# A hybrid trunk layer on one core: the opening laid out anew, and the operands of phase B made one by one

## The chip, the cores and the metric

One core of one Trainium2 chip runs the whole kernel. The metric is the device time of one execution in microseconds; the time of a kernel is the median over its runs.

## The reference

The layer normalises 16 learned meta tokens and 1024 tokens of width 2048, multiplies them with one combined weight `w_in` (2048 x 10240), and cuts the result into queries, keys, values, gates, the input of a pooling mixer, and two merge gates:

```python
h = rmsnorm(x, gain)
zin = h @ w_in.astype(h.dtype)
q, k, v, g_attn, u, g_pool, m_attn, m_pool = jnp.split(zin, cuts, axis=-1)
o_attn = stick_breaking_attention(q, k, v).reshape(B, L, SB_WIDTH)
y_attn = (o_attn * silu(g_attn)) @ w_attn_up
mixed = einsum(multiscale_pool(u), pool_w)
y_pool = (mixed * pool_scale * silu(g_pool)) @ w_pool_up
merged = sigmoid(m_attn) * y_attn + sigmoid(m_pool) * y_pool
return x + merged @ w_out
```

A second RMS norm with `final_gain` follows. The change touches only the way in which `zin` is computed; everything behind it is as before.

## The kernel before, in words

**Products.** Each fp32 operand is split into a hi and a lo part (`split`, L115: hi on ACT, lo on DVE or POOL), and a product is three matmuls: hi by hi, hi by lo, lo by hi (`mm3`, L137 to L140). The weight's parts are the tiles `wh` and `wl` (four buffers each, two products' worth), the tokens' parts are the X tiles.

**Pairs.** Two column blocks of 128 of `w_in` make a pair (class `Duo`); there are 40. The tokens are cut into two halves of 512 and the 2048 rows of the weight into two halves, and a pair's result is made with seven block products in place of eight, over sums of blocks. Phase A, per pair, does four products of 24 matmuls of 128x512: X0, X2, X1 and X3 are token-side operands. X0 and X1 hold the first half of the tokens, X2 and X3 differences with the last half. A pair's weight blocks arrive as four `raw` tiles of 512 KB (`load_raw`, L207; the first index `kh` is the half of the rows); POOL makes eight sums of them (`make_sums`, L221: r1 to r4, two of each), of which r2 and r3 go into X2's and X3's products, and r1 and r4 are stored to `d_r` for phase B. Phase B does the other three products of a pair, with operands Y0, Y1, Y2, which are other sums of token blocks.

**Opening (L271 to L408).** Eight blocks of 128 tokens and the 16 meta tokens are loaded, normed (`norm_block`, L276) and transposed on PE 128x128 at a time (`turn`, L314, tile `xtr`). Blocks 0 to 3 and meta become X0 and X1 (`first_tokens`). Blocks 4 to 7 go through `last_tokens` (L333): e22 (a scaled transpose, stored to `d_x22`), t3 (a difference), t2 (X0 less t3, two operations on POOL), then the splits of t3 into X3 and of t2 into X2. It is called 16 times with 256 columns: for blocks 4 and 5, then for blocks 6 and 7. The tiles of blocks 4 to 7 and of meta share two `xt` buffers in pool `p0`. Two pairs run in the opening: their X0 and X1 products between the steps of the norm, their X2 and X3 products at the end. Raw tiles and sums of these pairs come from `p0` too; the loop's come from pool `wa`, which opens when `p0` is closed.

**Loop (L441 to L464).** The other 38 pairs follow, with the next pair's raw tiles (raw0 four buffers, raw1 two) loaded and summed during the present pair. In eight of them `second_operands` (L418) makes 512 columns of two of phase B's operands on DVE: it fetches `d_x22` into an `st` tile (L422), subtracts X2, stores `d_t1`; and a second `st` tile gets a chain of three subtractions and additions that begins at L427, and is stored to `d_t4`. The same four `st` buffers carry the pairs' results to `d_nu`, `d_up`, `d_sa` and `d_sp`.

**Into phase B (L474 to L487).** 24 tiles of 512 columns are read back from `d_t1`, `d_t4` and `d_x22` through the four `wr` buffers and split, all of Y0, Y1 and Y2, before `duo` (L491) is called for the first pair.

**What sets the order.** A scheduler places each engine's instructions, which then run in that order and wait for semaphores. All DMAs are issued by one engine, SyncE, in its own order, and one that waits for a buffer holds back those behind it.

## Time and profile before

| | us |
|---|---|
| median of 3 runs | 2665.68 |
| lowest, highest run | 2661.87, 2668.41 |
| profiled execution, its time | 2664.01 |
| profiled execution, its span | 2662.3 |
| PE busy in the span | 2521.7 |
| phase A's last product ends | 1028.9 |
| phase B's first product starts | 1045.24 |

The profile is one execution; times count from the start of its span. PE is the matmul engine, DVE, ACT and POOL the elementwise ones, SP the one that issues the DMAs. A group of instructions is named by its line, engine, operation and tiles (without buffer numbers, so that r1 to r4 all read `r`), and idle time in front of an instruction is put down to what released it.

### The profile page before, as it was taken

The page shows a single profiled execution, that of the slowest core. Times are in us where ns is not written, and L with a number is a line of the kernel's source. Part 1 is how long each engine was busy: PE and PEld are TensorE (multiplying, and loading weights), DVE is VectorE, ACT ScalarE, POOL GpSimd, SP SyncE. Part 2 cuts the span into 40 slices and gives each one's busy share as a digit, 9 for nine tenths or more (in the row PEclk, how much of TensorE's full clock was granted, in tenths as well). Part 3 has the DMA queues.
Part 4 walks back from the last instruction along what each step waited for, and adds up shares of the span by engine and source line. Part 5 has one row for each costly group of instructions (what it writes and reads, how often), then busy time and mean ns, then how long its engine had stood idle before and what let it go on. Part 6 is the DMA issues. An engine that isn't in the chain of part 4 may idle for free.

```text
span 2662.3 us, 36486 instructions
## 1 busy us (share of the span) xinstructions
PE 2521.7 (95%) x12968; PEld 2123.3 (80%) x12968; DVE 1306.1 (49%) x2183; ACT 950.4 (36%) x1929; POOL 881.2 (33%) x802
## 2 busy tenths in 40 slices
PE   6589899999999997999999999999999999999998
PEld 5368677888888886888888888888778888788888
DVE  6643434343333345575665566556744424544432
ACT  5422222222222224324555454545532223322331
POOL 3555344554455452334323322333201101211010
PEclk9799999999999998999999999999999999999999
DMA  5455655555555556544334433433394434564431
GB/s 193 145 176 179 207 185 181 182 178 175 178 178 178 178 163 196 162 131 151 119 120 127 120 119 126 125 118 100 112 285 144 143 103 141 184 201 143 146 101 64
DMA packets 386775, 409.88 MB, mean 154 GB/s; under 512 B 34064, under 2 KB 262416, under 8 KB 385552
## 3 DMA queue, kind: packets, MB, share of 16 engines
q1 hardware_dynamic: 386592, 407.54, 48.4%
q8 instruction: 102, 1.67, 0.3%
q14 instruction: 81, 0.66, 0.1%
HBM read 298.17 MB, written 109.28 MB: 153 GB/s over the span
## 4 chain that ended last, share of the span: by engine, by line
PE 77%; DMA 6%; POOL 5%; DVE 5%; issue 3%; ACT 2%; SPq 1%; DVEq 0%; POOLq 0%; ACTq 0%
PE acc L138 15%; PE acc L139 15%; PE acc L140 15%; PE accb L826 4%; PE accb L825 4%; PE accb L824 4%; POOL r L226 4%; PE accb L140 4%; PE accb L138 4%; PE accb L139 4%; DMA raw<-in_w_in_dram 2%; PE tr L644 1%; DMA st<-d_x 1%; DVE bt L629 1%; PE av L139 1%
## 5 line engine op out<-in xcount | busy, mean ns | idle before, releaser
L138 PE MATMUL acc<-x,wh 128*128 128x512 f32 (+2 forms) x2736 | 979.0, 358 | 30.6 <-ACT wh L116 24.0
L140 PE MATMUL acc<-x,wl 128*128 128x512 f32 (+2 forms) x2736 | 975.4, 357 | 21.2 <-DVE wl L117 21.2
L139 PE MATMUL acc<-x,wh 128*128 128x512 f32 (+2 forms) x2736 | 975.2, 357 | 1.7 <-DVE x L117 1.7
L138 PEld LDWEIGHTS acc<-x,wh 128*128 128x128 f32 x2736 | 519.7, 190 | 106.2 <-ACT wh L116 26.7
L140 PEld LDWEIGHTS acc<-x,wl 128*128 128x128 f32 x2736 | 519.0, 190 | 101.7 <-DVE wl L117 28.2
L139 PEld LDWEIGHTS acc<-x,wh 128*128 128x128 f32 x2736 | 519.3, 190 | 72.6 <-DVE x L117 3.8
L116 ACT ACTIVATE wh<-wr 128x512 fp32r<-128x512 f32 x480 | 302.2, 630 | 512.2 <-PE accb L139 166.5
L117 DVE TENSOR_TENSOR wl<-wr,wh 128x512 fp32r<-128x512 f32 x360 | 258.9, 720 | 274.8 <-ACT wh L116 265.3
L117 POOL TENSOR_TENSOR wl<-wr,wh 128x512 fp32r<-128x512 f32 x120 | 171.3, 1427 | 364.6 <-ACT wh L116 265.5
L226 POOL TENSOR_TENSOR r<-raw,raw 128x512 f32<-128x512 f32 x80 | 115.2, 1440 | 411.5 <-DMA raw<-in_w_in_dram 390.6
L226 POOL TENSOR_TENSOR r<-r,raw 128x512 f32<-128x512 f32 x160 | 232.0, 1450 | 14.1 <-DMA raw<-in_w_in_dram 4.9
L116 ACT ACTIVATE wh<-r 128x512 fp32r<-128x512 f32 x160 | 101.0, 632 | 376.1 <-PE acc L139 183.8
L117 DVE TENSOR_TENSOR wl<-raw,wh 128x512 fp32r<-128x512 f32 x152 | 131.0, 868 | 207.0 <-ACT wh L116 192.7
L117 DVE TENSOR_TENSOR wl<-r,wh 128x512 fp32r<-128x512 f32 x160 | 151.1, 945 | 155.3 <-ACT wh L116 154.9
L140 PE MATMUL accb<-x,wl 128*128 128x512 f32 x512 | 201.2, 393 | 2.8 <-DVE wl L117 2.8
L138 PE MATMUL accb<-x,wh 128*128 128x512 f32 x512 | 200.9, 392 | 2.3 <-ACT wh L116 2.3
L139 PE MATMUL accb<-x,wh 128*128 128x512 f32 x512 | 200.2, 391 | 0.0
L116 ACT ACTIVATE wh<-raw 128x512 fp32r<-128x512 f32 x160 | 100.5, 629 | 244.1 <-PE acc L139 213.1
L826 PE MATMUL accb<-wl,x 128*128 128x512 f32 x448 | 175.9, 393 | 0.7 <-DVE wl L117 0.7
L824 PE MATMUL accb<-wh,x 128*128 128x512 f32 x448 | 175.8, 392 | 0.0
L825 PE MATMUL accb<-wh,x 128*128 128x512 f32 x448 | 175.7, 392 | 0.0
L816 POOL TENSOR_TENSOR sa<-sa,sp 128x512 f32<-128x512 f32 x32 | 51.0, 1592 | 319.4 <-DVE sa L815 310.1
(167 smaller groups left out, 3042.9 us busy)
## 6 DMA issues: line engine op xcount, KB each, us to landing
raw<-in_w_in_dram SPq DMA_DIRECT2D x104, 512.0 KB, 5.2
d_r<-r SPq DMA_DIRECT2D x160, 256.0 KB, 2.0
wr<-d_r SPq DMA_DIRECT2D x160, 256.0 KB, 2.9
raw<-in_w_in_dram SPq DMA_DIRECT2D x128, 256.0 KB, 5.3
wr<-in_w_out_dram SPq DMA_DIRECT2D x128, 256.0 KB, 2.6
wr<-in_w_in_dram SPq DMA_DIRECT2D x80, 256.0 KB, 3.0
wr<-in_w_pool_up_dram SPq DMA_DIRECT2D x64, 256.0 KB, 3.8
wr<-in_w_attn_up_dram SPq DMA_DIRECT2D x64, 256.0 KB, 3.4
```

The costliest lines, as they stand in the source:

```text
L116: nc.scalar.activation(hi, src, AF.Copy)
L117: (eng or nc.vector).tensor_tensor(out=lo, in0=src, in1=hi.bitcast(F32), op=ALU.subtract)
L138: nc.tensor.matmul(ps, wh, rh, start=first, stop=False, skip_group_check=skip)
L139: nc.tensor.matmul(ps, wh, rl, start=False, stop=False, skip_group_check=skip)
L140: nc.tensor.matmul(ps, wl, rh, start=False, stop=last, skip_group_check=skip)
L226: nc.gpsimd.tensor_tensor(out=t, in0=a, in1=b, op=ALU.add)
L629: nc.vector.tensor_tensor(out=bt[:, :w], in0=bt[:, :w], in1=wt[:, 1 : w + 1], op=ALU.mult)
L644: nc.tensor.transpose(tr[:, n, :], bt[:, off : off + P], ident)
L816: nc.gpsimd.tensor_tensor(out=sa, in0=sa, in1=sps.pop(c), op=ALU.add)
L824: nc.tensor.matmul(a, sh, wh, start=k == 0, stop=False)
L825: nc.tensor.matmul(a, sl, wh, start=False, stop=False)
L826: nc.tensor.matmul(a, sh, wl, start=False, stop=k == KC - 1)
```

## The change

1. The opening's `xt` tiles get a pool of their own, `px`, with four buffers, for blocks 4 to 7 and meta (five loads). `last_tokens` runs 8 times with 512 columns in place of 16 times with 256. Its tiles e22 and t2 have one buffer each, t3 is a `wr` tile, and the first operation on t2 moves from POOL to DVE. The squares' junk goes to `wr` tiles.
2. Three pairs run ahead in place of two. Their X0 and X1 products come first, with `last_tokens` put in between those of pairs 1 and 2 (two calls behind each half of their X1 products); the copies s1 of the first products are held in `wr` tiles. Their X2 and X3 products follow, with sums from `wa`, which takes the place of `px` in memory.
3. All raw tiles come from one pool `ws` and, for the last of a pair's four, from `wa`: raw0 has two buffers, raw1 one, rawb one.
4. `second_operands` works in `wr` tiles, and its `d_x22` is fetched one pair earlier by `fetch_x22`.
5. Y0, Y1 and Y2 are each made when `duo` first asks for them (`operand(n)`).

The diff, cut to its core:

```diff
-            def load_raw(pool, d, kh, kq, bufs):
-                raw = pool.tile([P, QD, 2 * P], F32, tag=f"raw{kh}", name=nm("raw"), bufs=bufs)
+            def load_raw(d, kh, kq, pool=None):
+                if pool is None:
+                    raw = ws.tile([P, QD, 2 * P], F32, tag=f"raw{kh}", name=nm("raw"), bufs=2 - kh)
+                else:
+                    raw = pool.tile([P, QD, 2 * P], F32, tag="rawb", name=nm("raw"), bufs=1)
...
+            early = ALL[:3]
...
-                        xt = p0.tile([P, D], F32, tag="xt", name=nm("xt"), bufs=2)
+                        xt = px.tile([P, D], F32, tag="xt", name=nm("xt"), bufs=4)
...
+                def last_tokens(r):
+                    tb, _ = turn(g2, r + KC // 2)
+                    e22 = p0.tile([P, HALF], F32, tag="e22", name=nm("e22"), bufs=1)
...
+                    t3 = wr_tile()
...
+                    t2 = p0.tile([P, HALF], F32, tag="t2", name=nm("t2"), bufs=1)
-                    nc.gpsimd.tensor_tensor(out=t2, in0=bh, in1=t3, op=ALU.subtract)
+                    nc.vector.tensor_tensor(out=t2, in0=bh, in1=t3, op=ALU.subtract)
                     nc.gpsimd.tensor_tensor(out=t2, in0=t2, in1=bl, op=ALU.add)
...
-                g2 = [norm_block(4), norm_block(5)]
+                g2 = [norm_block(b) for b in range(HB, NB)]
...
+                for d in early[1:]:
+                    early_ops(d, 0)
+                    a = acc_tile()
+                    for kq in range(KQ):
+                        block([a], WHOLE, X0, kq, ops[d.n, 0, kq], True)
+                    s1[d.n] = wr_tile()
+                    nc.scalar.activation(s1[d.n], a, AF.Copy)
+                    early_ops(d, 1)
+                    for kq in range(KQ):
+                        block([a], WHOLE, X1, kq, ops[d.n, 1, kq], False)
+                        for i in range(2):
+                            last_tokens(4 * (d.n - 1) + 2 * kq + i)
+                    out_c(p0, 2, d, [a], WHOLE)
...
-                return [[load_raw(wa, d, kh, kq, 4 - 2 * kh) for kq in range(KQ)] for kh in range(2)]
+                return [[load_raw(d, 0, 0), load_raw(d, 0, 1)], [load_raw(d, 1, 0), load_raw(d, 1, 1, wa)]]
+
+            for d in early:
+                raws = all_raws(d)
+                r2, r3 = make_sums(wa, d, raws, SB)
...
-                t = st_tile(wa, STB)
-                nc.sync.dma_start(t, d_x22[r])
+                t = x22s.pop(r)
...
-                t = st_tile(wa, STB)
+                t = wr_tile()
                 nc.vector.tensor_tensor(out=t, in0=f[1][0], in1=f[2][0], op=ALU.subtract)
...
+                if 3 <= n < 3 + KC // 2:
+                    fetch_x22(n - 3)
...
-            prod(c, pieces, Y0, lambda kq: d_r[d.n][0][:, kq * 512 : (kq + 1) * 512], True)
+            prod(c, pieces, operand(0), lambda kq: d_r[d.n][0][:, kq * 512 : (kq + 1) * 512], True)
...
-            prod(n4, pieces, Y1, lambda kq: w_in[krows(1, kq), d.c1 : d.c1 + P].rearrange("(k p) c -> p k c", p=P), True)
+            prod(n4, pieces, operand(1), lambda kq: w_in[krows(1, kq), d.c1 : d.c1 + P].rearrange("(k p) c -> p k c", p=P), True)
```

The order of the instructions at three places follows. First ACT in the opening, from the last squares of the norm on. `junk` is the squares of a block, `rs` the root of its norm, `wh` the hi part of a weight, `e22`, `t3` and `t2` the tiles of `last_tokens`, `st` and `wr` copies of results. Before, from the squares of block 5:

```order
L298 ACTIVATE junk_106_783,ssq_105_781<-xt_104_780 128x1024
L298 ACTIVATE junk_107_785,ssq_105_781<-xt_104_780 128x1024
L116 ACTIVATE wh_134_907<-raw_132_904 128x512
L149 ACTIVATE rs_109_790<-var_108_788 128x1
L245 ACTIVATE st_119_884<-acc_112_799 128x512
L263 ACT_TABLE_LOAD
L263 ACTIVATE st_120_886<-acc_69_572 128x256
L263 ACTIVATE st_120_886<-acc_70_573 128x256
L339 ACTIVATE e22_136_913<-xtr_135_910,gk_404 128x256
```

Now, from the squares of block 7:

```order
L309 ACTIVATE junk_122_827,ssq_121_825<-xt_120_824 128x1024
L309 ACTIVATE junk_123_829,ssq_121_825<-xt_120_824 128x1024
L267 ACT_TABLE_LOAD
L267 ACTIVATE st_128_891<-acc_70_579 128x256
L149 ACT_TABLE_LOAD
L149 ACTIVATE rs_125_834<-var_124_832 128x1
L116 ACTIVATE wh_139_906<-raw_137_903 128x512
L116 ACTIVATE wh_142_912<-raw_140_909 128x512
L116 ACTIVATE wh_147_945<-raw_145_942 128x512
L116 ACTIVATE wh_150_951<-raw_148_948 128x512
L388 ACTIVATE wr_144_940<-acc_143_915 128x512
L348 ACTIVATE e22_152_971<-xtr_151_966,gk_407 128x512
```

The first weights of pair 1 (`wh_139`) stand behind all of block 7's norm; before, pair 1's first weights were split earlier, ahead of the first row shown.

Second POOL, where the last tokens and the sums of the first pairs meet. Before:

```order
L226 TENSOR_TENSOR r2_260_1372<-r3_259_1370,raw_257_1366 128x512
L226 TENSOR_TENSOR r1_261_1374<-raw_255_1362,raw_257_1366 128x512
L226 TENSOR_TENSOR r4_262_1376<-r2_260_1372,raw_257_1366 128x512
L346 TENSOR_TENSOR t2_196_1130<-x0_1_393,t3_195_1128 128x256
L347 TENSOR_TENSOR t2_196_1130<-t2_196_1130,x0_2_394 128x256
L346 TENSOR_TENSOR t2_201_1148<-x0_1_393,t3_200_1146 128x256
L347 TENSOR_TENSOR t2_201_1148<-t2_201_1148,x0_2_394 128x256
L346 TENSOR_TENSOR t2_206_1166<-x0_1_393,t3_205_1164 128x256
L347 TENSOR_TENSOR t2_206_1166<-t2_206_1166,x0_2_394 128x256
```

Now, the sums being those of pair 0:

```order
L356 TENSOR_TENSOR t2_190_1147<-t2_190_1147,x0_4_399 128x512
L356 TENSOR_TENSOR t2_195_1169<-t2_195_1169,x0_4_399 128x512
L230 TENSOR_TENSOR r3_211_1248<-raw_207_1240 128x512
L230 TENSOR_TENSOR r1_213_1252<-raw_207_1240,raw_209_1244 128x512
L230 TENSOR_TENSOR r2_212_1250<-r3_211_1248,raw_209_1244 128x512
L230 TENSOR_TENSOR r3_215_1258<-raw_208_1242 128x512
L230 TENSOR_TENSOR r4_214_1254<-r2_212_1250,raw_209_1244 128x512
L356 TENSOR_TENSOR t2_200_1203<-t2_200_1203,x0_4_399 128x512
L230 TENSOR_TENSOR r2_216_1260<-r3_215_1258,raw_210_1246 128x512
L230 TENSOR_TENSOR r1_217_1262<-raw_208_1242,raw_210_1246 128x512
L230 TENSOR_TENSOR r4_218_1264<-r2_216_1260,raw_210_1246 128x512
L356 TENSOR_TENSOR t2_205_1225<-t2_205_1225,x0_4_399 128x512
```

The subtraction of t2 has left POOL, and the last two of its eight additions stand behind five and three of pair 0's sums.

Third ACT at the step into phase B (`x0`, `x1`, `x2` are now Y0, Y1, Y2; `wr` and `ym` what is read back). Before:

```order
L116 ACTIVATE x1_1632_8744<-wr_1668_8870 128x512
L116 ACTIVATE x1_1632_8744<-ym_1669_8874 128x16
L481 ACTIVATE x2_1634_8746<-wr_1670_8878 128x512
L481 ACTIVATE x2_1634_8746<-wr_1671_8882 128x512
L481 ACTIVATE x2_1634_8746<-wr_1672_8886 128x512
L481 ACTIVATE x2_1634_8746<-wr_1673_8890 128x512
L481 ACTIVATE x2_1636_8748<-wr_1674_8894 128x512
L481 ACTIVATE x2_1636_8748<-wr_1675_8898 128x512
L481 ACTIVATE x2_1636_8748<-wr_1676_8902 128x512
L481 ACTIVATE x2_1636_8748<-wr_1677_8906 128x512
L116 ACTIVATE pwh_1678_8916<-wr_1680_8918 128x512
L116 ACTIVATE wh_1689_8935<-wr_1687_8932 128x512
```

Now:

```order
L116 ACTIVATE wh_1588_8608<-r3_1563_8460 128x512
L116 ACTIVATE x0_1601_8666<-wr_1615_8716 128x512
L116 ACTIVATE x0_1601_8666<-wr_1617_8724 128x512
L116 ACTIVATE x0_1601_8666<-ym_1618_8728 128x16
L116 ACTIVATE wh_1621_8735<-wr_1619_8732 128x512
L116 ACTIVATE x1_1628_8798<-ym_1633_8806 128x16
L116 ACTIVATE x1_1628_8798<-ym_1635_8814 128x16
L116 ACTIVATE wh_1624_8765<-wr_1622_8762 128x512
L267 ACTIVATE st_1584_8600<-acc_1568_8497 128x512
L116 ACTIVATE x1_1628_8798<-wr_1632_8802 128x512
```

Phase B's first weights (`wh_1689` before, `wh_1621` now) stand right behind the last tiles of Y0, and Y1's tiles behind them.

More of the change, by code (lines that the diff above doesn't have):

```diff
@@ L294, in norm_block @@
                     for i, hh in enumerate(halves):
-                        on_act = i == 0 or b not in (0, 1)
-                        junk = p0.tile([P, D // 2], BF16, tag="junk" if on_act else "st", name=nm("junk"), bufs=1 if on_act else 3)
-                        if on_act:
+                        junk = wp.tile([P, D // 2], BF16, tag="wr", name=nm("junk"), bufs=4)
+                        if i == 0 or b not in (0, 1):
                             nc.scalar.activation(junk[:n], xt[:n, hh], AF.Square, accum_out=ssq[:n, i : i + 1])
@@ L349, in last_tokens @@
-                    split(X2[kq][0][:, j, cs], X2[kq][1][:, j, cs], t2)
-                early = ALL[:2]
+                    split(X3[kq][0][:, j], X3[kq][1][:, j], t3)
+                    split(X2[kq][0][:, j], X2[kq][1][:, j], t2)
                 half = [range(0, KC // 2), range(KC // 2, KC)]
                 g0 = [norm_block(0), norm_block(1)]
-                ops = {}
-                raws = {}
-                def early_ops(d, kh):
-                    for kq in range(KQ):
-                        raw = load_raw(p0, d, kh, kq, 2 - kh)
-                        ops[d.n, kh, kq] = op_of(c0(raw), nc.gpsimd)
@@ L398, in trunk_kernel @@
[L398 to L402 removed]
+                out_c(p0, 2, early[0], A0, SPLIT)
+                X2, X3 = xquads(2, HALF), xquads(3, HALF, xp)
+                for d in early[1:]:
+                    early_ops(d, 0)
+                    a = acc_tile()
@@ L472, in load_wr, with operand @@
             return raw
-        Y0, Y1, Y2 = xquads(0, XW), xquads(1, XW), xquads(2, HALF)
-        for Y, src, neg in ((Y0, d_t1, False), (Y1, d_t4, False), (Y2, d_x22, True)):
+        Y = {}
+        def operand(n):
+            if n in Y:
+                return Y[n]
+            Y[n] = xquads(n, XW if n < 2 else HALF)
+            src = (d_t1, d_t4, d_x22)[n]
             for r in range(KC // 2):
@@ L523, in duo @@
             out_of((1, 0), n4, up, False)
-            prod(c, SPLIT if d.meta else WHOLE, Y2, lambda kq: d_r[d.n][1][:, kq * 512 : (kq + 1) * 512], False)
+            prod(c, SPLIT if d.meta else WHOLE, operand(2), lambda kq: d_r[d.n][1][:, kq * 512 : (kq + 1) * 512], False)
             out_of((0, 1), c, nu, True)
```

77 lines of the change are left out of this document (29 added, 48 removed).

## The prediction, made before the result was known

> **What bounds the kernel now.** I read the page's busy table first, then the sums over stretches, then the waits of PE, then PE's timeline at the longest waits.
>
> ```profile
> span 2662.3 us, 36486 instructions
> ...
> PE 2521.7 (95%) x12968; PEld 2123.3 (80%) x12968; DVE 1306.1 (49%) x2183; ACT 950.4 (36%) x1929; POOL 881.2 (33%) x802
> ```
>
> PE is busy for 2521.7 of 2662.3 us, and the change takes no matmul of the products away. So all it can give lies in the 140.6 us in which PE stands idle, and in what the lower clock behind such gaps costs. Where these lie, the sums over stretches tell (the columns are PE, PEld, DVE, ACT, POOL busy, granted PE clock, DMA share, GB/s):
>
> ```profile
> 50.30:75.00 24.70, 17.61 (x80) 12.89 (x78) 14.55 (x23) 13.58 (x29) 17.38 (x17) 0.90 0.47 152
> 75.00:101.30 26.30, 4.78 (x18) 3.15 (x18) 18.53 (x31) 12.36 (x26) 16.81 (x17) 0.51 0.60 188
> 101.30:143.70 42.40, 28.43 (x112) 18.60 (x112) 18.08 (x34) 10.18 (x24) 15.70 (x18) 0.98 0.31 106
> 262.10:489.70 227.60, 208.37 (x866) 164.72 (x865) 91.05 (x130) 53.27 (x90) 101.69 (x74) 0.98 0.56 190
> 489.70:1005.00 515.30, 515.30 (x2779) 445.04 (x2778) 200.35 (x230) 140.86 (x266) 267.62 (x187) 1.00 0.56 175
> 1005.00:1055.00 50.00, 33.63 (x168) 28.77 (x167) 26.89 (x55) 25.00 (x56) 4.98 (x5) 0.83 0.73 224
> ```
>
> Three places lose time, and the change touches all three: the opening (7.1, 21.5 and 14.0 us idle up to 143.7), the pairs from 262 to 490 (19.2 us), and the step into phase B (16.4 us). From 490 to 1005 PE never waits. PE's waits over the whole run, then its timeline at the gaps (idle time and releaser in brackets):
>
> ```profile
> PE xtr L320 <- DVE xt L308: 36.8, 5, 16.1
> PE acc L138 <- ACT wh L116: 24.0, 3, 16.4
> PE acc L140 <- DVE wl L117: 21.2, 14, 2.4
> ```
>
> ```profile
> 91.95 1.09 PE L320 MATMUL xtr<-ident,xt 128*128 128x128 f32 x4 [16.10 <-DVE xt L308]
> 97.64 3.01 PE L320 MATMUL xtr<-ident,xt 128*128 128x128 f32 x12 [4.60 <-DVE xt L308]
> ...
> 143.74 0.79 PE L138 MATMUL acc<-x,wh 128*128 128x512 f32 x1 [7.36 <-ACT wh L116]
> ...
> 168.59 0.40 PE L138 MATMUL acc<-x,wh 128*128 128x512 f32 x1
> ...
> 217.69 0.40 PE L138 MATMUL acc<-x,wh 128*128 128x512 f32 x1
> ...
> 239.90 0.40 PE L138 MATMUL acc<-x,wh 128*128 128x512 f32 x1
> ...
> 489.66 0.29 PE L138 MATMUL acc<-x,wh 128*128 128x256 f32 x1
> ...
> 1028.47 0.40 PE L140 MATMUL acc<-x,wl 128*128 128x512 f32 x1
> 1045.24 0.58 PE L138 MATMUL acc<-x,wh 128*128 128x256 f32 x1 [16.37 <-ACT wh L116]
> ```
>
> The rows without a bracket are starts of pairs: pair 3 at 168.59, pairs 5 and 6 at 217.69 and 239.90 (an undisturbed pair takes 22.21 us, a product 5.55), the first u pair, number 16, at 489.66. The sum below is made against the profiled execution, 2664.0 us; the median of the runs lies 1.7 us above it, well inside their spread of 6.5.
>
> **Part 1, the opening: 20 us.** The waits of 16.10 and 4.60 us are for blocks 6 and 7, whose loads stand behind the two shared buffers. With four buffers blocks 4 to 6 come early, and block 7 takes the buffer of meta. In the chain of waits of before block 5's load stands so, and ACT at that time:
>
> ```profile
> 46.64 5.81 DMA xt<-in_x_dram
> ```
>
> ```profile
> 52.53 1.06 ACT L298 ACTIVATE junk<-xt 128x1024 bf16<-128x1024 f32 x1 [2.86 <-DMA xt<-in_x_dram]
> 53.50 0.19 ACT L298 ACTIVATION_READ_ACCUMULATOR junk<-xt 128x1 f32 x1
> 56.71 1.28 ACT L263 ACT_TABLE_LOAD   x1
> ```
>
> The last of four blocks lands about where block 5 does now, near 52.5. Its squares now stand on ACT ahead of pair 1's first operands: two times 1.25, two table loads of 1.28, a copy, a root and the split (0.63 by a row below) put that split's end near 59. PE has only transposes from 50.5 until then, so this is a new wait of some 6.5 us; pair 1's first product ends near 66. Then last_tokens runs in 8 rounds of 512 columns. One t2 buffer makes the rounds a chain, which I price by the 512-column rows of 50 to 147 us, and 256-column ones beside them:
>
> ```profile
> L346 POOL TENSOR_TENSOR t<-x,t 128x256 f32<-128x256 f32 x16 | 13.6, 852 | 8.0 <-DVE t L343 8.0
> L226 POOL TENSOR_TENSOR r<-r,raw 128x512 f32<-128x512 f32 x8 | 11.8, 1481 | 0.2 <-DMA raw<-in_w_in_dram 0.2
> ...
> L117 DVE TENSOR_TENSOR wl<-r,wh 128x512 fp32r<-128x512 f32 x8 | 8.2, 1030 | 3.7 <-ACT wh L116 3.6
> L343 DVE SCALAR_TENSOR_TENSOR t<-xtr,gk,e 128x256 f32<-128x256 f32 x16 | 7.2, 475 | 2.0 <-ACT e L339 2.0
> ...
> L116 ACT ACTIVATE wh<-r 128x512 fp32r<-128x512 f32 x8 | 4.9, 625 | 6.5 <-PE acc L139 5.0 <-POOL r L226 1.4
> ```
>
> A round is subtract 1.03 (DVE, moved there from POOL), add 1.48 (POOL), hi 0.63 (ACT), lo 1.03 (DVE) and four hand-overs of 0.2, so 5.0 us. The 0.2 is the gap in this row of DVE:
>
> ```profile
> 101.30 0.66 DVE L117 TENSOR_TENSOR x<-t,x 128x256 fp32r<-128x256 f32 x1 [0.20 <-ACT x L116]
> ```
> The first t3 is there near 68, and the add of the sixth round ends near 95.5. Then POOL has five sums of pair 0 (7.4 us), the add of round 7, three more sums (4.4) and the add of round 8, which ends near 110; hi and lo follow, and pair 0's X2 product ends near 113, its X3 at 118.5. SyncE's queue has the fourth raw tile of pair 0 behind the last transposes, but POOL is still busy when it lands. Pairs 1 and 2 are paced by load, sums and product in turn. A raw tile takes 4.8 us to land:
>
> ```profile
> raw<-in_w_in_dram SPq DMA_DIRECT2D x62, 512.0 KB, 4.8
> d_r<-r SPq DMA_DIRECT2D x63, 256.0 KB, 2.0
> ```
>
> The first raws of a pair wait for the sums of the one before, its last one also for the nu store. So pair 1's two products end near 131, pair 2's X2 starts near 134.5 (2 sums after its raws), and its X3 ends near 147, in place of 168.59. That is 21.6; I take 20, for half clock behind one more gap. Bounds: 8 if each round costs 1.5 us more (a POOL operation in between), and 47 if only PE were left (10 products of 5.55 and 64 transposes of 0.25 after 50.3 end at 122). The value lies near the low end because the chain of rounds is known by its rows.
>
> A rule speaks of that clock. After the wait of 7.36 us the first matmul takes 0.79 us, and 0.40 in pair 5. The Trainium skill (TensorE: Matmul & The Clock Gate, What's actually happening) says that an idle window of about 3.4 us halves the clock, until one such window has been busy. By it each of my three gaps (59, 100, 134) would cost up to 1.7 us, an estimate from that page, and the end would be 3.4 us later than mine; the trace agrees on the halving and not on the length, since 4.60 us of idle near 97 were followed by a stretch at 0.98.
>
> **Part 2, pairs 3 to 15: 31 us.** From 168.59 to 489.66 stand 321.1 us; thirteen undisturbed pairs are 288.7, so 32.4 are lost, in the nine pairs of 262 to 490 above all (25.3 each). DVE waits there:
>
> ```profile
> DVE wl L117 <- ACT wh L116: 52.7, 31, 2.5
> DVE st L427 <- DMA d_sp<-st: 35.7, 4, 9.1
> DVE st L427 <- DMA d_sa<-st: 34.7, 4, 8.8
> ```
>
> L427 is the first subtraction of t4 in second_operands: it waits for an st tile whose store is late, 8.8 us each time, and the lo splits of the next products stand behind it on DVE; PE then waits for wl 14 times. With wr tiles that wait has no object, since a slot comes round after two rounds, and d_x22 is fetched a pair ahead. What is late next would be the raws, and they have slack: the four wl buffers let X1's operands be split two products ahead, so raw1 is free near +5 and +7.5 us of a pair and lands again near +12.3; its sums (six of 1.48) are done near +21.2, and the next pair's r2 is needed at 22.2 + 5.6 = 27.8. So 22.2 us a pair; I leave 1.4 of 32.4 for one slow clock window. Bounds 15 (second operands still cost half) and 33.
>
> **Part 3, into phase B: 9 us.** The last X3 ends at 1028.9, the next product starts at 1045.24: 16.4 us idle, and 2.3 (an estimate: some 5 us of work at half clock, by the 0.83 granted there), 18.7 lost. In that stretch:
>
> ```profile
> L116 ACT ACTIVATE x<-wr 128x512 fp32r<-128x512 f32 x16 | 10.0, 625 | 6.4 <-DMA wr<-d_t 4.7 <-PE acc L140 1.8
> L481 ACT ACTIVATE x<-wr 128x512 fp32r<-128x512 f32 x8 | 5.0, 630 | 5.4 <-DMA wr<-d_x 5.3
> ```
>
> 24 tiles go through ACT before the first weights: 15.0 us of work and 11.8 of waiting for loads, 1.1 us a tile. After, the first weights stand behind 8 tiles only, which are ready before X3 ends. The other 16 need 1.1 us each, or 1.5 (four thirds of it) while pool_w holds one of four wr slots, from about 1027 on: 1045 to 1051. PE's three products of 5.6 need until 1046, and each waits for the tiles of its operand. The third product ended near 1064 (1045.24, three of 5.6, 2.3 for the clock); now it ends between 1047 and, with a last half product and a slow clock behind the last tile, 1055. I take 1055, since every load of these tiles shares SyncE's queue: 9. Bounds 3 (the tiles wait on each other as now) and 17.
>
> Costed at nothing: the junk of the squares in wr tiles, which nothing else uses by then, and the doubled raw of the first three pairs, which POOL's earlier work hides; if that cover is gone, it is in the 1.5 us a round of part 1's lower bound.
>
> **Sum.** 20 + 31 + 9 = 60: 2664.0 - 60 = 2604, and 2605 against the median.
>
> **The rivals.**
>
> *DVE and POOL block each other (0.12).* The lo split takes 1.03 us here, beside 0.69 where POOL rests:
>
> ```profile
> L117 DVE TENSOR_TENSOR x<-wr,x 128x512 fp32r<-128x512 f32 x16 | 11.0, 688 | 5.4 <-ACT x L116 5.2
> ```
>
> If each of three two-input DVE operations in a round (t2 and two lo) had to wait for a whole POOL one, 1.48 in place of the mean 0.34, 8 rounds would take 8 x 3 x 1.14 = 27 us more, and 20 gained become 7 lost: 2632. Against it speaks that mean, a quarter of an operation. The Trainium skill (SBUF — State Buffer, Who interferes with whom) states this rule for two-input DVE operations beside POOL reads, the later one fully blocked; the trace agrees on some operations only.
>
> *The second operands still block (0.15).* The scheduler pulls them into pairs 3 to 7, and DVE now waits for the d_x22 fetch instead. A third of part 2 remains: 2625. For it: the SyncE queue is in order. Against it: the fetch is issued early.
>
> *Slower: the single raw buffers (0.07).* If a raw tile lands later than 11.4 us after issue (4.8 and the slack of 6.6 us, 27.8 less 21.2), every one of 37 pairs waits. At the 3.1 us that a disturbed pair loses now (25.3 less 22.2), 37 pairs lose 115: 2719. Against it: the raws landed in 4.8.
>
> *The opening near PE's own time (0.06).* Rounds that overlap: 27 us more, 2577.
>
> *It does not do what it says (0.05).* The chain of rounds and the sums behind it take back what the other parts give: about 2660.
>
> **How the numbers follow.** The forecast has 0.55; the range 2585 to 2635 holds it with its bounds and the first two rivals, 0.82, and leaves out the last three. A measurement can tell about 0.3%, 8 us, from no change. Faster by more: 0.55 + 0.12 + 0.15 + 0.06 = 0.88; within: 0.05; slower: 0.07.
>
> **What would show it.** Right: in the changed profile no wait for xt of over 3 us near 90; PE starts pair 3 near 147; pairs 3 to 15 take 22.2 us; no gap near 1029, and waits of 10 us in all until 1055. Wrong: waits of PE for r or raw in every pair, DVE rows of 1.5 us and more in the rounds, or a wait for wl in pairs 3 to 7.

## The result, and the profile after

| | us | ratio to before (95% interval) |
|---|---|---|
| before, median | 2667.05 (2661.87 to 2669.29) | |
| after, median of 4 runs | 2625.99 (2621.62 to 2632.07) | 0.985 (0.9825 to 0.9875) |
| profiled execution of after, its time and span | 2632.07, 2630.4 | |

The kernel became faster by 41 us in the medians and by 31.9 us between the two profiled spans; the profile after is of the slowest of its four executions. One execution of a repeat of after took 3110 us at a granted clock of 0.749, and no figure below contains it. The result lies in the range, 21 us above the forecast of 2605. The page of after begins so:

```profile
span 2630.4 us, 36376 instructions
...
PE 2522.7 (96%) x12968; PEld 2130.9 (81%) x12968; DVE 1317.9 (50%) x2163; ACT 948.8 (36%) x1907; POOL 883.4 (34%) x782
```

PE does the same work (2522.7 us, before 2521.7), so the gain is idle time. The stretches of after, cut nearly as those of before (PE, PEld, DVE, ACT, POOL busy, granted PE clock, DMA share, GB/s):

```profile
0.00:50.30 50.30, 30.26 (x149) 24.05 (x149) 30.65 (x83) 30.27 (x68) 6.56 (x10) 0.83 0.66 222
50.30:75.00 24.70, 17.41 (x80) 13.45 (x80) 11.63 (x26) 16.30 (x28) 7.32 (x6) 0.79 0.41 120
75.00:101.30 26.30, 22.10 (x111) 17.86 (x109) 17.26 (x23) 13.60 (x23) 12.91 (x9) 0.94 0.52 171
101.30:120.00 18.70, 8.59 (x21) 5.54 (x21) 18.00 (x18) 5.44 (x10) 16.05 (x12) 0.73 0.59 193
...
170.00:262.00 92.00, 78.71 (x313) 62.31 (x312) 62.33 (x86) 19.09 (x33) 40.38 (x27) 0.93 0.63 208
262.00:490.00 228.00, 228.00 (x1033) 187.20 (x1032) 93.01 (x103) 61.68 (x107) 123.70 (x85) 1.00 0.53 178
...
1005.00:1037.30 32.30, 23.07 (x150) 22.20 (x150) 19.77 (x31) 15.50 (x28) 5.24 (x4) 0.84 0.84 265
```

From 75 to 101 PE now works 22.1 us where it worked 4.8, and from 262 to 490 it never waits. But two holes have grown: 10.1 us idle from 101 to 120 (5.7 in before), and 13.3 us idle from 170 to 262 (2.7 in before). PE's timeline at the starts of pair 4 (180.39), pair 7 (267.03) and the first u pair, number 16 (466.95), with the gaps between and behind them:

```profile
62.49 0.80 PE L138 MATMUL acc<-x,wh 128*128 128x512 f32 x1 [2.52 <-ACT wh L116]
...
107.23 0.79 PE L138 MATMUL acc<-x,wh 128*128 128x512 f32 x1 [6.47 <-ACT wh L116]
...
180.39 0.40 PE L138 MATMUL acc<-x,wh 128*128 128x512 f32 x1
194.23 0.65 PE L140 MATMUL acc<-x,wl 128*128 128x512 f32 x1 [2.18 <-DVE wl L117]
...
218.33 0.79 PE L140 MATMUL acc<-x,wl 128*128 128x512 f32 x1 [3.44 <-DVE wl L117]
...
253.65 0.80 PE L140 MATMUL acc<-x,wl 128*128 128x512 f32 x1 [5.79 <-DVE wl L117]
...
267.03 0.40 PE L138 MATMUL acc<-x,wh 128*128 128x512 f32 x1
...
466.95 0.29 PE L138 MATMUL acc<-x,wh 128*128 128x256 f32 x1
...
1015.99 0.38 PE L138 MATMUL acc<-x,wh 128*128 128x256 f32 x1 [4.00 <-ACT wh L116]
1029.09 0.58 PE L138 MATMUL acc<-x,wh 128*128 128x256 f32 x1 [5.23 <-ACT wh L116]
...
1037.14 0.40 PE L138 MATMUL acc<-x,wh 128*128 128x512 f32 x1
```

The last row is the fourth product of phase B; in before it stood here:

```profile
1064.75 0.40 PE L138 MATMUL acc<-x,wh 128*128 128x512 f32 x1
```

Pairs 7 to 15 take 466.95 - 267.03 = 199.9 us, nine times 22.21, the undisturbed pair. Pair 3 ran without a gap, so its start is put at 180.39 - 22.21 = 158.2 (its X0 product is interleaved with the opening's last). That gives the parts:

| | before | after | gain | forecast |
|---|---|---|---|---|
| opening, until pair 3 starts | 168.6 | 158.2 | 10.4 | 20 |
| pairs 3 to 15 | 321.1 | 308.8 | 12.3 | 31 |
| first u pair until phase A's last product ends (1028.86, 1006.15) | 539.2 | 539.2 | 0 | 0 |
| step into phase B, until its fourth product | 35.9 | 31.0 | 4.9 | 9 |
| the rest | 1597.5 | 1593.3 | 4.3 | 0 |

The last row is no work of the change. From the matmul at 1141.9 in before to the start of the last one stand 1511.5 us; the same stretch, counted in matmuls from the end, takes 1507.5 in after and from 1507.2 to 1512.4 in the other kernels profiled below, with 1508.1 in the fastest of all and 1511.3 in the one from which it differs by a queue.

Pairs 3 to 6 take 108.8 us and not 88.8: 20 us are lost there, 13.3 of them idle time and the rest the slow clock behind it (0.65 to 0.80 us for a matmul of 0.40 in the rows above). What DVE and then SyncE's queue wait for, from 160 to 270:

```profile
DVE tm L437 <- DMA d_t<-tm: 15.6, 4, 6.5
DVE wr L426 <- DMA wr<-d_x: 8.4, 1, 8.4
```

```profile
SPq L239 <- POOL r L230: 47.6, 19, 4.8
```

L426 and L437 are lines of `second_operands`: its first subtraction, from the fetched d_x22, and the sum of 16 meta columns in a `tm` tile, of which there are four. SyncE at L239 issues the stores of r1 and r4 to `d_r`, and each waits in the queue for POOL's sum. The sums in turn wait for raw loads out of the same queue (51.6 us in four waits of POOL, from 160 to 270). Two single waits show the chain, first DVE, then SyncE's queue before the second of them:

```profile
192.07 0.18 DVE L437 TENSOR_TENSOR tm<-x,x 128x16 f32<-128x16 f32 x1 [6.47 <-DMA d_t<-tm]
...
251.57 1.42 DVE L426 TENSOR_TENSOR wr<-wr,x 128x512 f32<-128x512 f32 x2 [8.41 <-DMA wr<-d_x]
```

```profile
242.64 0.32 SPq L239 DMA_DIRECT2D d_r<-r  x1
...
245.05 0.38 SPq L216 DMA_DIRECT2D raw<-in_w_in_dram  x1
245.49 0.68 SPq L419 DMA_DIRECT2D wr<-d_x  x1
```

The fetch that DVE needs at 243.2 is issued only at 245.49, behind the stores and raw loads, and lands 6 us later. DVE stands still, with lo splits of the next product behind it.

### The profile page after: what moved, and what is told of

Read it like the earlier page. It is cut to its first block, busy times and chain, and to the rows that moved or that the text cites. A ratio compares the mean times of both kernels' runs of the same rounds, so it can differ in the third digit from the quotient of the medians.

```text
span 2630.4 us, 36376 instructions
## 1 busy us (share of the span) xinstructions
PE 2522.7 (96%) x12968; PEld 2130.9 (81%) x12968; DVE 1317.9 (50%) x2163; ACT 948.8 (36%) x1907; POOL 883.4 (34%) x782
## 4 chain that ended last, share of the span: by engine, by line
PE 81%; DVE 4%; issue 2%; DMA 2%; ACT 1%; POOL 0%; DVEq 0%; SPq 0%; POOLq 0%; ACTq 0%
PE acc L139 17%; PE acc L138 17%; PE acc L140 17%; PE accb L837 4%; PE accb L836 4%; PE accb L835 4%; PE accb L138 4%; PE accb L140 4%; PE accb L139 4%; PE tr L655 1%; DVE bt L640 1%; PE av L139 1%; PE av L140 1%; DVE wt L639 1%; PE av L138 1%
## 5 line engine op out<-in xcount | busy, mean ns | idle before, releaser
L230 POOL TENSOR_TENSOR r<-r,raw 128x512 f32<-128x512 f32 x160 | 248.0, 1550 | 11.6 <-DMA raw<-in_w_in_dram 3.1
```

Of the source, the lines that this page charges most:

```text
L230: nc.gpsimd.tensor_tensor(out=t, in0=a, in1=b, op=ALU.add)
```

## The experiments

The medians of all runs, with the start of the first u pair in each profile (before 489.66, after 466.95). Before was run again beside each, at 2663 to 2667.

| kernel | median us | ratio (95% interval) | first u pair |
|---|---|---|---|
| after, repeated (3 runs) | 2629.51 | 0.9873 (0.985 to 0.9895) | |
| before with part 5 alone | 2661.15 | 0.9987 (0.9975 to 0.9998) | 497.06 |
| before with part 4 alone | 2647.92 | 0.9929 (0.9904 to 0.9954) | 477.63 |
| after without parts 4 and 5 | 2650.73 | 0.9938 (0.9918 to 0.9958) | 479.78 |
| after, 16 tm buffers | 2633.33 | 0.9894 (0.987 to 0.9918) | 463.89 |
| after, d_r stored by POOL | 2631.08 | 0.9877 (0.9858 to 0.9895) | 462.93 |
| after, packed raw tile | 2623.12 | 0.9845 (0.983 to 0.9859) | 458.94 |
| packed, two rawb buffers | 2635.56 | 0.9885 (0.987 to 0.9899) | 468.85 |
| packed, second operands' DMAs by ACT | 2629.9 | 0.9863 (0.9847 to 0.988) | 461.63 |
| packed, tm columns in wr tiles | 2629.19 | 0.9861 (0.9844 to 0.9877) | 464.66 |
| the same, one round per pair | 2621.92 | 0.9837 (0.9821 to 0.9853) | 453.98 |
| the same, d_r stored by POOL | **2611.34** | 0.9786 (0.977 to 0.9803) | 444.09 |

**After, repeated**, with no edit.

> The changed kernel once more, for a second profile and times beside the others. Its first profiled execution was its slowest (2632.1 against a median of 2626.0). If that is scatter in the first 60 us (pair 0's X1 product ended at 54.1 there, 50.3 in the kernel before), this one starts pair 7 three to five us sooner than 267.0 and takes 2624 to 2628; the stretch from pair 3 to pair 7 keeps its 108.7 us, if the waits in it belong to the order and not to scatter.

The three executions read 2625.8, 2629.51 and 2635.32, and there is no second profile of after. So after lies between 2622 and 2635, and a difference of 5 us between two of these kernels decides little by itself: the profiles have to tell.

### The parts one by one

**Part 5 alone**: Y0, Y1, Y2 made when first asked for, on the kernel before.

```diff
-        Y0, Y1, Y2 = xquads(0, XW), xquads(1, XW), xquads(2, HALF)
+        Y = {}
+        def operand(n):
+            if n in Y:
+                return Y[n]
...
```

> The kernel before with part 5 alone: Y0, Y1, Y2 made one by one. In the changed kernel everything behind the last X3 product became 9.0 us shorter (1624.4 in place of 1633.4). Theory (the parts add up): 9 us here too, a ratio near 0.9965, with waits of 4 to 5 us for Y1 and for Y2 in place of the one of 16.4. Rival: the gain needs the wr slots and the earlier stores of the changed kernel; then 4 us or less.

Measured: 2661.15. From phase A's last product to the fourth of phase B stand 31.5 us, 4.4 less than before, and 3.1 came in the rest; ahead of it all, the profile is 7.4 longer, though nothing was edited there. Most of that, 6.2, is there when X1 of pair 0 ends (56.65 against 50.50), with the slow clock at the start that the last section tells of. So part 5 alone shows about the 4.9 of after, and not the 9 that were expected.

**Part 4 alone**: the second operands in `wr` tiles, d_x22 fetched a pair ahead, on the kernel before.

```diff
-                t = st_tile(wa, STB)
-                nc.sync.dma_start(t, d_x22[r])
+                t = x22s.pop(r)
...
-                t = st_tile(wa, STB)
+                t = wr_tile()
...
+                if 3 <= n < 3 + KC // 2:
+                    fetch_x22(n - 3)
```

> The kernel before with part 4 alone: second operands in wr tiles, d_x22 fetched a pair ahead. Theory (queue): the scheduler may put the eight rounds as early as their inputs are there, into three or four pairs, where DVE waits for tm slots and fetches behind the d_r stores; of the 32 us that pairs 3 to 15 lose before, 17 to 22 stay lost, so 10 to 15 us gain. Rival (my prediction): the waits go, and the gain is 25 or more.

Measured: 2647.92, in the profile the first u pair 12.0 us earlier. Pair 3 starts at 178.42, 9.8 us later than in before; 8.1 of these are there when X1 of pair 0 ends (58.60), again with the slow clock at the start. Pairs 3 to 15 then take 299.2 us: 10.5 are lost, 8.6 of them in pair 3, against 20 in after and 32.4 before. The 21.9 won in the pairs lie between the two expectations. Two of its stretches, and then its start of phase B:

```profile
150.00:262.00 112.00, 102.24 (x412) 81.25 (x413) 53.26 (x77) 28.96 (x48) 56.02 (x40) 0.93 0.64 204
262.00:490.00 228.00, 228.00 (x1014) 186.40 (x1013) 94.43 (x104) 61.77 (x104) 118.66 (x82) 1.00 0.56 185
```

```profile
1033.71 0.58 PE L138 MATMUL acc<-x,wh 128*128 128x256 f32 x1 [16.88 <-ACT wh L116]
```

The idle time of 262 to 490 is gone here too, and part of it has moved ahead of 262. The wait into phase B stays at 16.88 us, as it should without part 5.

**Without parts 4 and 5**: after, with the second operands in `st` tiles and Y0 to Y2 made at once, so parts 1 to 3 alone.

```diff
-                t = x22s.pop(r)
+                t = st_tile(wa, STB)
+                nc.sync.dma_start(t, d_x22[r])
...
-            prod(c, pieces, operand(0), lambda kq: d_r[d.n][0][:, kq * 512 : (kq + 1) * 512], True)
+            prod(c, pieces, Y0, lambda kq: d_r[d.n][0][:, kq * 512 : (kq + 1) * 512], True)
```

> The changed kernel with the second operands in st tiles and the three Y at once, as before: parts 1 to 3 alone. Theory (the parts add up): pair 3 starts some 10 us sooner than in the kernel before (168.6), the pairs behind it lose their 32 us as before, and the last part has its 18.7: a gain of 8 to 14 us in all. Rival (raw buffers): the one buffer of raw1 and rawb delays loads in these pairs, and they lose more than before; then less than 5, or nothing.

Measured: 2650.73. Pair 3 starts at 155.36, so the opening gains 13.2 us by itself, with the clock of the first 50 us at 0.93 as in before; the pairs behind it lose 35.7, 3.3 more than before, and the first u pair comes 9.9 us earlier. What DVE waits for in its pairs:

```profile
DVE st L424 <- DMA d_sp<-st: 37.2, 4, 11.7
DVE st L424 <- DMA d_sa<-st: 34.8, 4, 9.1
```

These are the waits of before (35.7 and 34.7). The medians of the three kernels lie 4, 17.5 and 14.7 us below before, 36 in all; the whole change gave 34 to 41. By the medians the parts add up. By stages they do not quite: pairs 3 to 15 gain 21.9 us with part 4 alone and 12.3 with all parts, the opening 13.2 with parts 1 to 3 and 10.4 with all, and the profiles differ in the clock at their start (0.93 in the first 50 us with parts 1 to 3, 0.76 with part 4 alone, 0.83 with all).

### Why pairs 3 to 6 lose 20 us

The theory from the profile is SyncE's order: what DVE waits for stands behind stores that wait for POOL. Its rivals are too few buffers (tm, raw), and the load itself, eight rounds packed into four pairs.

**16 tm buffers.** If the four `tm` tiles are the cause, more of them end the loss; if SyncE's order is, the wait moves.

```diff
...
-                    tm = wa.tile([P, META], F32, tag="tm", name=nm("tm"), bufs=4)
+                    tm = wa.tile([P, META], F32, tag="tm", name=nm("tm"), bufs=16)
```

> Sixteen tm buffers in place of four, all else as changed. Theory (queue): DVE waits in pairs 3 to 6 for the slots of tm, whose small stores stand on SyncE behind the d_r stores that wait for POOL's sums; with a slot for each the three waits of 6.5, 3.4 and 4.3 us go, the fourth (8.4 us, for the last fetch of d_x22) stays, and the stretch from pair 3 to pair 7 falls from 108.7 to 96 to 100 us, the whole by 9 to 12. Rival (load): DVE simply has too much to do in these pairs (62 of 92 us busy, eight rounds in four pairs); then the waits move to the next operation and the stretch stays above 105.

Measured: 2633.33. No DVE wait for a tm store is left, and this stands in its place (150 to 470):

```profile
DVE wr L426 <- DMA wr<-d_x: 21.3, 5, 8.1
```

Pairs 3 to 6 take 106.8 us, 2 less than in after and above 105, as the rival had it. The buffers only chose the place of the wait.

**d_r stored by POOL.** The 160 stores that wait for POOL's sums leave SyncE's queue.

```diff
-                        nc.sync.dma_start(d_r[d.n][m][:, kq * 512 : (kq + 1) * 512], r.rearrange("p k c -> p (k c)"))
+                        nc.gpsimd.dma_start(d_r[d.n][m][:, kq * 512 : (kq + 1) * 512], r.rearrange("p k c -> p (k c)"))
```

> The d_r stores are issued by POOL, which makes the sums, and not by SyncE. Theory (queue): SyncE then never waits for POOL (47.6 us in pairs 3 to 6 now), all four waits of DVE go, and the stretch from pair 3 to pair 7 falls from 108.7 to 89 to 93 us; the opening gains a few us too, as raw loads leave earlier; 2600 to 2610 in all. Rival (cost of issue on POOL): each of the 160 stores costs POOL 1 us or more, and beside 11.6 us of sums and its other work in a pair of 22.2 that pushes the sums back; then pairs after 7 are longer than 22.2, and the whole is no faster than the changed kernel.

Measured: 2631.08. DVE's waits in 160 to 270, and the stretches up to 262:

```profile
DVE tm L437 <- DMA d_t<-tm: 2.8, 1, 2.8
DVE wr L426 <- DMA wr<-d_x: 0.4, 1, 0.4
```

```profile
147.00:170.00 23.00, 10.61 (x36) 7.75 (x35) 19.48 (x23) 1.56 (x4) 14.76 (x14) 0.70 0.77 258
170.00:262.00 92.00, 89.90 (x387) 72.24 (x386) 64.36 (x83) 24.41 (x41) 52.66 (x46) 1.00 0.70 228
```

The waits for DMAs are gone (24.0 to 3.2), and pairs 4 to 6 take 69.4 us, 2.8 above undisturbed ones. But ahead of 170 PE now idles 12.4 of 23 us, with DVE busy for 19.5: the rounds, no longer held up, crowd together at the end of the opening, the lo splits stand behind them, and pair 3 starts at 171.38, 13.2 us later than in after. The cause of the waits is shown; the time did not follow.

**Packed raw tile.** In the opening, the two quarters of a pair's second half of rows share one raw1 tile, in place of taking the one raw1 buffer in turn, and only the 128 of 256 columns that are used are loaded.

```diff
-                for kq in range(KQ):
-                    ops[d.n, kh, kq] = op_of(c0(load_raw(d, kh, kq)), nc.gpsimd)
...
+                raw = ws.tile([P, QD, 2 * P], F32, tag="raw1", name=nm("raw"), bufs=1)
+                for kq in range(KQ):
+                    nc.sync.dma_start(raw[:, :, kq * P : (kq + 1) * P], w_in[krows(kh, kq), d.c0 : d.c0 + P].rearrange("(k p) c -> p k c", p=P))
...
```

> Of the early pairs' second halves only the 128 columns that are used are loaded, both quarters into one raw1 tile, so the second quarter waits for no slot. Theory (raw slot): in the changed kernel the split of pair 1's fourth weight waits until 71.4 us for a load that waits for the one raw1 slot, and e22 of the first round of last tokens stands behind it on ACT; here the first e22 comes at 67 to 68 in place of 72.4, and pair 3 starts 4 to 6 us sooner. Rival (chain): POOL and DVE, which slow each other down in the rounds, set the end anyway; then pair 3 starts within 1.5 us of before.

Measured: 2623.12. Pair 4 starts at 174.33 in place of 180.39, so pair 3 near 152.1. The 6 us are the size that the theory named, but 3.9 of them are there already when pair 1 starts (58.60 against 62.49), as in the kernels in which the clock was not slow at the start. Pairs 3 to 6 still take 106.9 (pair 7 starts at 259.02). The raw tile belongs to the opening's account, below, and not to this one. The next five kernels build on this one.

**Two rawb buffers**, in case the raw loads hold the queue.

```diff
-                    raw = pool.tile([P, QD, 2 * P], F32, tag="rawb", name=nm("raw"), bufs=1)
+                    raw = pool.tile([P, QD, 2 * P], F32, tag="rawb", name=nm("raw"), bufs=2)
```

> The kernel pack1 with two buffers for the last of a pair's four raw tiles. Part 4 alone won back 24 of the 32 us of pairs 2 to 15, in a kernel with twice the raw buffers; the changed kernel won 12. Theory (raw buffers don't matter): pairs 3 to 15 stay within 3 us of pack1's 306.6. Rival (raw buffers): loads, sums and d_r stores come earlier, SyncE is held up less, and these pairs take 300 or less.

Measured: 2635.56, 12 us slower than with one, the first u pair at 468.85. DVE waits 19.8 us for tm stores, and pairs 3 to 15 take 312.0 us, more than either expectation had. The single raw buffers are not what the pairs wait for.

**The second operands' DMAs issued by ACT**: the d_x22 fetches and the d_t1 and d_t4 stores leave SyncE's queue in place of the d_r stores.

```diff
-                nc.sync.dma_start(x22s[r], d_x22[r])
+                nc.scalar.dma_start(x22s[r], d_x22[r])
...
```

> The kernel pack1 with all DMAs of the second operands issued by ACT and not by SyncE. Theory (queue): no DMA of theirs stands behind a d_r store, so DVE waits for none of them by more than 2 us, and pairs 4 to 6 take 22.2 each (19 us less than in pack1). Rival (load): the scheduler then packs the eight rounds into the end of the opening and pair 3, where POOL makes sums and two-input DVE operations take 1.7 us and more; PE then waits 10 us or more there, as it did from 152 to 165 us with the d_r stores on POOL, and the whole is within 8 us of pack1.

Measured: 2629.9, 7 us more than with packing alone. DVE's waits for these DMAs fell to 6.2 us in all, and again the rounds crowded into the end of the opening and pair 3; PE waits 11.5 us for `st` (L254, copies that DVE makes). So a second cause stands beside SyncE's order: eight rounds being placed in so short a time. How many are placed there shows in DVE's groups from 100 to 267, of after:

```profile
L426 DVE TENSOR_TENSOR wr<-wr,x 128x512 f32<-128x512 f32 x16 | 13.1, 821 | 8.6 <-DMA wr<-d_x 8.4
```

Two such subtractions are a round, so all eight rounds lie ahead of pair 7 (one in the opening, seven in pairs 3 to 6); the source names pairs 7 to 14. The scheduler places an instruction where its inputs and its buffer are there, and with `wr` tiles they are.

**tm columns in the wr tiles**: the two small tiles stand beside d_x22 in one wider wr tile, so that a round needs no `tm` slot.

```diff
-                x22s[r] = wr_tile()
-                nc.sync.dma_start(x22s[r], d_x22[r])
+                w = wp.tile([P, XW + META], F32, tag="wr", name=nm("wr"), bufs=4)
+                x22s[r] = w[:, :HALF], w[:, HALF:]
+                nc.sync.dma_start(w[:, :HALF], d_x22[r])
...
-                    tm = wa.tile([P, META], F32, tag="tm", name=nm("tm"), bufs=4)
+                    tm = tm2[:, i * META : (i + 1) * META]
```

> The kernel pack1 with the sixteen extra columns of the second operands in the same wr tile as the other 512 (544 columns wide), so that their small operations wait for its slot. Theory (crowding in the opening): in the changed kernel seven such 128x16 operations stand among the last rounds of last tokens and take 1.2 us each there, beside POOL's sums, where they take 0.16 alone; with most of them gone pair 3 starts 3 to 5 us sooner than in pack1 (152.3). Rival (POOL): sums and additions on POOL set that time, and pair 3 starts within 1.5 us of pack1. Pairs 3 to 6 keep their waits under both.

Measured: 2629.19. The opening ends no sooner, and DVE waits 17.2 us for d_x22 and 7.9 for stores in its pairs: the waits moved once more, as with 16 buffers.

**One round per pair.** The first copy s1 of the loop's first twelve pairs (3 to 14) takes a wr tile too, so that a slot comes free once per pair and the scheduler cannot place the rounds closer.

```diff
-                s1 = copy_p1(wa, STB, a, pieces)
+                s1 = copy_p1(wa, STB, a, pieces, wr_tile() if n < 12 else None)
```

> The kernel tmw with the pairs' s1 copies in the wr ring too, from pair 3 to 14. Their slots come free only as pairs end, so the ring deals out the second operands at one round a pair, in pairs 6 to 14, in place of eight rounds in four pairs. Theory (packing is the cost): the waits of pairs 3 to 6 go, a round hides in its pair, and pairs 3 to 15 take 289 to 297 us in place of 306.6 in pack1; with the opening of tmw some 2600 to 2612 in all. Rival (every round costs a wait, as before the change, where the pairs with a round took 25.3): 8 rounds at 3 us, 313 us for pairs 3 to 15, and no gain over pack1.

Measured: 2621.92, and the first u pair at 453.98, 10.7 us earlier than without. Its groups from 100 to 267, then DVE's waits and SyncE's:

```profile
L434 DVE TENSOR_TENSOR wr<-wr,x 128x512 f32<-128x512 f32 x4 | 3.9, 974 | 7.7 <-DMA wr<-d_x 7.7
```

```profile
DVE wr L434 <- DMA wr<-d_x: 39.3, 8, 6.4
```

```profile
SPq L239 <- POOL r L230: 183.4, 45, 6.9
```

Two rounds in place of eight lie ahead of 267, and pairs 3 to 6 are undisturbed. But each round still waits for its fetch, 39.3 us in eight waits, now spread over pairs 6 to 13, which lose 0 to 4 us each. From pair 4 (173.31) to the first u pair stand 280.7 us, 14.2 above twelve undisturbed pairs; pairs 3 to 15 take 302.9, between the 289 to 297 of the theory and the 313 of the rival. The edit also takes s1 out of the four `st` buffers, and no run separates that from the pace.

**The same, with d_r stored by POOL.** Only the queue is taken away here: the edit is that of the stores above.

> This is the kernel with paced rounds (early quarters packed in one raw tile, one round of second operands per pair, tm columns beside d_x22 in the wr tile), with the stores of d_r issued by POOL in place of SyncE. Theory that the fetches of d_x22 stand on SyncE behind d_r stores that wait for POOL's sums: DVE's 39.3 us of waits for d_x in eight rounds falls to under 10, pairs 3 to 15 take 292 to 296 us in place of some 303, the first u product starts near 445, and the time is about 2613 us. Rival, that the rounds cost their pairs by the work itself (subtractions on DVE ahead of the copies and lo splits, DVE operations slowed beside POOL): the waits of DVE for d_x go but PE's waits of 2 to 3 us for st stay, the first u product starts near 453, and the time is 2620 to 2624. Second rival, that 160 more issues on POOL (0.56 us each) make its sums late: the first u product starts after 460, and the time is over 2627.

Measured: 2611.34 (2607.05 to 2611.97), which the queue theory had at 2613, and the fastest of all. Its DVE waits of 150 to 455, its stretches, and pair 4 and the first u pair on PE:

```profile
DVE wr L434 <- DMA wr<-d_x: 3.2, 4, 1.5
```

```profile
170.00:262.00 92.00, 92.00 (x400) 74.62 (x399) 48.39 (x55) 25.25 (x42) 59.24 (x53) 1.00 0.56 188
262.00:440.00 178.00, 178.00 (x771) 144.44 (x770) 105.34 (x132) 48.28 (x80) 113.97 (x98) 1.00 0.63 213
```

```profile
177.53 0.40 PE L138 MATMUL acc<-x,wh 128*128 128x512 f32 x1
...
444.09 0.29 PE L138 MATMUL acc<-x,wh 128*128 128x256 f32 x1
```

444.09 - 177.53 = 266.6 us, twelve times 22.21: no pair loses anything. Against before: 13.3 gained in the opening (pair 3 at 155.3), 32.3 in the pairs, 7.8 behind them, 53.4 in all, against 60 forecast for the change.

## Why the prediction was right or wrong, by its own steps

**The sum.** The time fell into the range, but the sum of 60 did not come. In the two profiles the three terms gave 27.6 us, and 4.3 more came from a stretch that the change does not touch. Part 2 lies below its own lower bound of 15. The range held the result because it was drawn wide enough for the rivals.

**Part 3: the mechanism was right, its size half.** Phase B's first product now follows phase A's last without a gap, and Y1 and Y2 wait 4.00 and 5.23 us, 9.2 in all where "waits of 10 us in all" were named. But of the 9 us 4.9 came, within the bounds of 3 to 17. The term that was too small is the clock behind the waits: the products behind the two gaps take 7.9 and 8.2 us (1015.99 to 1023.86, 1029.09 to 1037.30), and 6.0 the first, which had none. The forecast counted 2.3 for half clock in before, where one gap stood. Its 1055 names a slow clock behind the last tile, but 10 us of waits and three products of 5.6 fill the time from 1028.9 until then, so nothing was left for the clock behind two gaps.

**Part 2: the mechanism holds, and one step of it failed.** The forecast said of the wait for an st tile: "With wr tiles that wait has no object, since a slot comes round after two rounds, and d_x22 is fetched a pair ahead." The old wait did go. But what a fetch "a pair ahead" means is settled by the order of SyncE's queue, where it stands behind stores that wait for POOL; and the free tiles let the scheduler bring the eight rounds forward, ahead of pair 7, where the waits of DVE fall upon the same four pairs. Of 31 us 12.3 came. Each cause was taken away alone, and alone it was not enough: without the stores in the queue the rounds crowd the opening's end (2631), with one round per pair each still waits for its fetch (2622). Both together give the 22.2 us a pair that the forecast had worked out. That undisturbed pairs run at 22.2 with single raw buffers was right as well, and the rival of the single raw buffers fell: pairs 7 to 15 take exactly that, and another buffer did not help.

**The rival nearest to the result was "The second operands still block"**: it named DVE waiting for the d_x22 fetch in SyncE's order, and 2625. Its 2625 is 20 us above the forecast, so it had a third of part 2's gain remain; 12.3 of 31 remained, two fifths. That the median then fell 1 us from its time is luck: in the profile, at 2632, the opening gave 10 less and phase B 4 less besides. What it had "against it: the fetch is issued early" is what the queue undid: 245.49 for a fetch needed at 243.2.

**Part 1: the chain of rounds was right, its start and its end were not.** The second operation of t2 starts on POOL at 76.65, 81.82, 87.00, 91.63, 96.86 and 100.80, 4.8 us a round where 5.0 was worked out. But the sixth of them ends at 102.37 (forecast 95.5), the eighth at 119.93 (forecast 110), and pair 3 starts at 158.2 (forecast 147): 7, 10 and 11 us late. The first round starts 5 us late. ACT there:

```profile
61.83 1.66 ACT L116 ACTIVATE wh<-raw 128x512 fp32r<-128x512 f32 x3
71.40 0.63 ACT L116 ACTIVATE wh<-raw 128x512 fp32r<-128x512 f32 x1 [7.92 <-DMA raw<-in_w_in_dram]
...
72.41 0.68 ACT L348 ACTIVATE e<-xtr,gk 128x512 f32<-128x512 f32 x1
```

A split of pair 1's weights waits for a raw tile that itself waits for the one raw1 buffer, and e22 of the first round stands behind it. The doubled raw of the first pairs had been "costed at nothing", with POOL's work as its cover; the load of the next tile was overlooked. But this wait is not what makes the round late. PE ends the product ahead of e22's transposes at 71.16 and the transposes at 71.59, so it costs 0.8 us at most; and in the kernel with 16 tm buffers the same wait stands, with 7.96 us, and the first e22 comes at 67.55. What differs between the two is the clock. X1 of pair 0 ends at 54.10, and at 49.21 with 16 tm buffers (50.50 in before); the granted clock of the first 50 us was 0.83, 0.97 and 0.93. Then pair 1's X0 product, which the forecast had end near 66, starts at 62.49 behind gaps of 3.28 and 2.52 us and takes 8.67 us, most of it at half clock, and not 5.55. So the term that failed first is again the slow clock, for which 1.6 us had been taken off. The packed tile does take the raw wait away: from pair 1's first product to pair 3 stand 93.5 us there and 95.7 in after, so it is worth 2.2 of its 6.1 us.

The end is late too: pair 0's X3 ends at 132.3 (forecast 118.5), and DVE beside POOL's sums looks so:

```profile
105.31 1.75 DVE L355 TENSOR_TENSOR t<-x,wr 128x512 f32<-128x512 f32 x1
106.99 1.75 DVE L117 TENSOR_TENSOR x<-wr,x 128x512 fp32r<-128x512 f32 x1
...
113.26 1.25 DVE L437 TENSOR_TENSOR tm<-x,x 128x16 f32<-128x16 f32 x1
...
117.53 0.68 DVE L355 TENSOR_TENSOR t<-x,wr 128x512 f32<-128x512 f32 x1
```

The rival of DVE and POOL blocking each other was right here, and wrong for the rounds before, whose period stayed at 4.8. Small operations of the pulled-forward second operands stand among them. They are not the main cost: six of 128x16 stand between 95 and 125 with packing alone, three with the tm columns in wr tiles, none with one round per pair, and pair 3 starts at 152.12, 153.05 and 151.10. (With 16 tm buffers there are 24, and there pair 1 starts 4.9 us sooner than in after and pair 3 only 1.0.) What the blocked operations of 512 columns cost, no experiment separates; it stays open, as does why part 4 alone lost only 10.5 us in its pairs, and how the 13.3 of the opening in the fastest kernel compares with the packed one's 16.5 (its PE waits 7.30 us for a lo split at 112.73).

Two readings in the forecast's part 1 were off besides. From 134.5, two products of 5.55 end at 145.6 and not 147. And the clock behind the 4.60 us gap was not full: from 97.64 to 101.30, the stretch right behind it, 0.58 was granted, so this gap does not speak against the length of the window that is quoted there.

**It does what it says**, and the forecast's signs hold in part: PE has no wait for xt of over 3 us near 90 (one of 3.28 us is left, at 58.85), no gap stands at the last X3, and the waits behind it are 9.2 us; but only pairs 7 to 15 take 22.2, and pair 3 starts 11 us late. Two of the signs named as wrong came: "a wait for wl in pairs 3 to 7", with 2.18, 3.44 and 5.79 us at 194, 218 and 254, and DVE rows of 1.5 us and more in the rounds, in two of the eight subtractions of t2 (1.62 at 73.91, 1.75 at 105.31).

## What to carry to other kernels

A freed buffer does not only end a wait: it lets the scheduler bring the work forward, and where it lands has to be read from the order before the gain is counted. A load "issued early" is early only if nothing ahead of it in its queue waits for a slow engine: put stores that wait for a computation on another queue than the loads that others wait for. Where taking away one cause moves the wait and not the time, look for the second before giving the first up, and count the slow clock behind each gap that remains.
